# A hybrid encoder block on one core: 128-column sums and shifted work in the opening, value stores issued by ScalarE

## The chip, the core and the metric

The kernel runs on one core of a Trainium2 chip. The core has five engines that run side by side: TensorE (PE; its weight loads are listed apart as PEld), VectorE (DVE), ScalarE (ACT), GpSimd (POOL) and SyncE (SP), which only issues DMAs. Each engine works through its own queue in order and waits on semaphores for the others. The metric is the device time of one execution in microseconds; lower is better. Tiles lie in SBUF (128 partitions), TensorE writes into PSUM banks of 128 x 512 floats.

## The reference

One layer of an encoder on a sequence of 1024 positions with 1024 channels, all in float32. What bears on the change is the start of it:

```python
ada = silu(c) @ w_ada + b_ada                    # 6 x 1024 numbers from one vector c
shift1, scale1, gate1, shift2, scale2, gate2 = split(ada, 6)
h = rmsnorm(x, g_mix) * (1 + scale1) + shift1    # x: 1024 positions x 1024 channels
qa, ka, va, qb, kb, vb, ga, gb = split(h @ w_in)
oa = mixture_of_dilations(qa, ka, va)            # windows at dilations 1, 4 and 16, merged
ob = neighbourhood_attention_2d(qb, kb, vb)
x = x + gate1 * ((sigmoid(ga) * (oa @ w_branch_dil) + sigmoid(gb) * (ob @ w_branch_na)) @ w_out)
# then a second rmsnorm with shift2 and scale2, a ConvFFN, and a final rmsnorm
```

rmsnorm divides each position by the root of the mean of the squares over its 1024 channels.

## The kernel before

Activations lie transposed, channels on partitions and positions along the row, in two halves of 512 positions; a half of x is eight tiles of 128 x 512. A product in float32 precision is made of three: every operand is split into a rounded part (hi) and a rest (lo), and hi x hi, lo x hi and hi x lo are added up in PSUM. ScalarE makes hi, and GpSimd or VectorE subtracts to get lo (`split`, L57 and L61).

The part that the change touches comes first in the program, in a block with `manual_schedule`, in which the engines take their instructions in the order of the program text. Outside such blocks a planner orders them.

**The sums over channels.** A sum over the 128 partitions is a product with a column of ones. `add_sums` (L98) does this for the sums of squares, `ada_sums` (L160) for the rows of w_ada: in four products a 128 x 128 block is the stationary operand and a single column the moving one, so that one column comes out of each. In float32 every such product becomes two instructions. `warm` (L236) issues products of a 128 x 128 tile of ones with itself, whose results nobody reads; they stand between the sums.

**The opening.** c and the first half of x (8 tiles) are loaded first, then the blocks of w_ada, `wt[0]` to `wt[3]`, each of eight rows of 128 x 512, with the first weights of q, k (`qk_raw`) and v (`v_raw`) between them, and the second half of x after them, all by SP in this order. ScalarE squares the tiles of x, VectorE adds them (L452), TensorE sums over channels (`pcol`), and the reciprocal root r goes through transposes (`bcast`, L111) into a broadcast tile `pb`, which ScalarE copies to SBUF as `pbs` (L470). x is multiplied by it: tiles 0 and 1 on VectorE (L473), 2 and 3 on VectorE after the first bias (L481), 4 to 7 on GpSimd (L487).

**Rows of w_ada.** Of the eight rows of a block, some are multiplied by their number of silu(c) and added up on VectorE into one tile (`ada_rows`, L174 and L176), and that tile is summed over channels by TensorE with ones; the others go to TensorE as they are, with silu(c)'s column as the moving operand. All end in the PSUM tile `pada`.

**Four pieces.** Piece q of the loop `for q in range(4)` handles channel tiles 2q and 2q+1. `piece_bias(q)` takes the sums from `pada` (L293 adds b_ada, reading PSUM; L295 makes the scale `am1` from two SBUF operands), `scaled` makes hi and a full copy on ScalarE (L229, L230) and lo on VectorE (L231), `qk_products` (L310) adds this piece's share of q and k for the first pair of heads (12 instructions of 512 columns), and `v_parts` (L320) its share of v (24 of 256 columns). In between, VectorE works on the rows of the next block of w_ada, so that its sum is there for the next piece.

**The value stage.** After the pieces come the rest of v's first half, the second half of x (`modulate`), and the loop over `v_steps`, in which `v_wide` (L279 to L281) makes the values of 128 positions in 24 products of 512 columns into one of three PSUM banks `pv`. `v_out` copies a result to one of two SBUF tiles `vs` (ScalarE, L286) and stores it to DRAM by SP (L287). In the same loop VectorE works through the remaining blocks of w_ada in pairs of rows (`row_pairs`, L551 and L553, reloaded by L135 on SP), `row_ends` says how far by each step, and `due` when a block's sum goes to TensorE and its bias to VectorE (L167): two steps later. The fourth step splits the weights of the second branch's values, makes q and k of the second half, and copies the stored values into chunks (`va_chunks`, L408 and L410). After the loop come the sums that are left; then the buffers are freed and the attention's tables and values are loaded into them (first use of a table: L755 on GpSimd, L658 on VectorE).

The rest (attention with gates and projections beside it, branch and output projections, a ConvFFN with a seven-product scheme, the last norm) is not edited.

## Time and profile before

| what | value |
|---|---|
| plain runs, median of 3 | 1506.31 us (1505.19, 1506.31, 1511.78) |
| profiled execution, its own time | 1512.37 us |
| its span, first to last instruction | 1510.6 us |
| TensorE busy, share of the span | 1483.4 us, 98% |
| VectorE, ScalarE, GpSimd busy | 62%, 51%, 50% |
| mean granted TensorE clock | 0.992 |

Busy shares are of the whole span. For one stage one reads the timeline (start and duration of instructions, in brackets the idle time before one and what ended it), the chain of waits (the work that ended last, followed back from the end), and the stretches (busy time of an engine and the granted clock, PEclk, between two times; 1.00 is full speed). Where several instructions of a kind follow each other, a row has their count (x8), and its duration is that of all of them together. A line number can be that of a helper, so the tile's name goes with it.

### The profile page before, as it was taken

What the parts mean: (1) busy time and instruction counts of PE and PEld (TensorE: products, weight loads), DVE (VectorE), ACT (ScalarE), POOL (GpSimd) and SP (SyncE); (2) the same over time, 40 slices, a digit from 0 to 9 for tenths busy, and PEclk for the clock granted to TensorE, in tenths of its full rate; (3) what the DMA queues carried; (4) which work ended last, traced back from release to release, by engine and by line L of the source; (5) the groups of instructions that cost most, each with busy time, mean ns of one, the idle gap of its engine ahead of it and who ended that gap; (6) DMA issues with size and microseconds to landing.
All of it is one profiled execution on the core that took longest, in us unless ns stands there. A gap on an engine that the chain in (4) does not pass through costs nothing.

```text
span 1510.6 us, 21652 instructions
## 1 busy us (share of the span) xinstructions
PE 1483.4 (98%) x7664; PEld 1259.5 (83%) x7664; DVE 936.3 (62%) x1763; ACT 772.9 (51%) x1442; POOL 757.1 (50%) x633
## 2 busy tenths in 40 slices
PE   9999999999999999999999999999999999999997
PEld 8887888889798998888888778888888888777887
DVE  6684446464545665566515897666666668786765
ACT  4531666666655566653345464444444448465442
POOL 2221333433234454512268678766666676777621
PEclk8999999999999999999999999999999999999999
DMA  9477333434745555577644213222222232631323
GB/s 371 178 258 255 90 108 77 146 92 133 181 131 152 142 164 165 172 246 252 198 157 142 93 46 137 84 84 84 84 84 84 85 133 91 210 130 49 114 57 112
DMA packets 117300, 210.28 MB, mean 139 GB/s; under 512 B 42788, under 2 KB 55716, under 8 KB 117156
## 3 DMA queue, kind: packets, MB, share of 16 engines
q1 hardware_dynamic: 116632, 208.57, 43.2%
q8 instruction: 60, 0.98, 0.3%
q14 instruction: 48, 0.39, 0.1%
q10 hardware_dynamic: 560, 0.33, 0.1%
HBM read 163.58 MB, written 42.66 MB: 137 GB/s over the span
## 4 chain that ended last, share of the span: by engine, by line
PE 77%; DMA 7%; DVE 6%; POOL 4%; ACT 2%; issue 2%; SPq 0%; DVEq 0%; POOLq 0%; ACTq 0%
PE pj L1307 10%; PE pj L1306 10%; PE pj L1305 10%; PE pj L84 10%; PE pj L86 10%; PE pj L85 10%; PE pj L402 3%; PE O L1013 2%; POOL wsl L61 1%; DMA wraw<-w_down 1%; PE T L1000 1%; DMA fb<-fcs 1%; PE S L978 1%; PE O L844 1%; DMA big<-as 1%
## 5 line engine op out<-in xcount | busy, mean ns | idle before, releaser
L61 POOL TENSOR_TENSOR wlo<-wraw,whi 128x512 fp32r<-128x512 f32 (+1 forms) x96 | 118.0, 1251 | 167.6 <-ACT whi L57 152.7
L84 PE MATMUL pj<-h,whi 128*128 128x512 f32 x432 | 178.2, 413 | 0.4 <-DVE kl L374 0.4
L86 PE MATMUL pj<-h,wlo 128*128 128x512 f32 x432 | 169.8, 393 | 0.0
L85 PE MATMUL pj<-h,whi 128*128 128x512 f32 x432 | 169.4, 392 | 0.0
L1305 PE MATMUL pj<-op,wsh 128*128 128x512 f32 x408 | 159.3, 390 | 1.1 <-ACT op L1236 0.6
L1306 PE MATMUL pj<-op,wsh 128*128 128x512 f32 x408 | 158.8, 390 | 0.9 <-DVE op L1237 0.6
L1307 PE MATMUL pj<-op,wsl 128*128 128x512 f32 x408 | 158.1, 390 | 0.7 <-POOL wsl L61 0.7
L667 DVE TENSOR_TENSOR tl<-T,th 128x512 fp32r<-128x512 f32 (+3 forms) x120 | 77.1, 654 | 102.0 <-ACT th L666 100.9
L717 POOL TENSOR_TENSOR wlo<-wraw,whi 128x512 fp32r<-128x512 f32 x58 | 74.2, 1290 | 126.2 <-ACT whi L716 126.1
L61 POOL TENSOR_TENSOR wsl<-big,wsh 128x512 fp32r<-128x512 f32 (+1 forms) x86 | 113.3, 1339 | 45.2 <-ACT wsh L57 39.7
L659 ACT ACTIVATE P<-P,st 128x256 f32<-128x256 f32 x128 | 64.2, 502 | 94.2 <-DVE st L658 94.2
L1538 DVE SCALAR_TENSOR_TENSOR big<-pj,sm,big 128x512 f32<-128x512 f32 (+2 forms) x183 | 94.9, 563 | 16.5 <-ACT big L1532 15.5
L86 PEld LDWEIGHTS pj<-h,wlo 128*128 128x128 f32 x432 | 81.1, 188 | 18.1
L1305 PE MATMUL pj<-op,whi 128*128 128x512 f32 x232 | 91.3, 393 | 3.1 <-ACT whi L57 3.1
L57 ACT ACTIVATE whi<-wraw 128x1024 fp32r<-128x1024 f32 (+2 forms) x51 | 49.5, 972 | 84.2 <-DMA wraw<-w_down 32.2
L1307 PE MATMUL pj<-op,wlo 128*128 128x512 f32 x232 | 91.2, 393 | 1.3 <-POOL wlo L61 1.3
L1305 PEld LDWEIGHTS pj<-op,wsh 128*128 128x128 f32 x408 | 76.6, 188 | 18.7 <-ACT wsh L57 1.5
L1307 PEld LDWEIGHTS pj<-op,wsl 128*128 128x128 f32 x408 | 76.6, 188 | 17.9 <-POOL wsl L61 2.2
L1306 PEld LDWEIGHTS pj<-op,wsh 128*128 128x128 f32 x408 | 76.6, 188 | 17.7 <-DVE op L1237 1.3
L84 PEld LDWEIGHTS pj<-h,whi 128*128 128x128 f32 x432 | 81.5, 189 | 11.5 <-issue 0.8
L1306 PE MATMUL pj<-op,whi 128*128 128x512 f32 x232 | 90.6, 391 | 0.0
L85 PEld LDWEIGHTS pj<-h,whi 128*128 128x128 f32 x432 | 81.7, 189 | 10.1
(392 smaller groups left out, 4176.2 us busy)
## 6 DMA issues: line engine op xcount, KB each, us to landing
wraw<-w_in SPq DMA_DIRECT2D x32, 512.0 KB
wada<-w_ada SPq DMA_DIRECT2D x31, 512.0 KB
big<-w_up SPq DMA_DIRECT2D x22, 512.0 KB
wraw<-w_up SPq DMA_DIRECT2D x22, 512.0 KB
big<-as SPq DMA_DIRECT2D x22, 512.0 KB
as<-big SPq DMA_DIRECT2D x21, 512.0 KB
wraw<-w_down SPq DMA_DIRECT2D x24, 384.0 KB
gs<-gs SPq DMA_DIRECT2D x32, 256.0 KB
```

The source lines that it names most:

```text
L57: act.activation(hi, raw, AF.Copy)
L61: lo_eng.tensor_tensor(lo[:, i:i + step], raw[:, i:i + step], f(hi)[:, i:i + step], OP.subtract)
L84: pe.matmul(psum, whi[:, k0 + k], mhi, start=k == 0, stop=False)
L85: pe.matmul(psum, whi[:, k0 + k], mlo, start=False, stop=False)
L86: pe.matmul(psum, wlo[:, k0 + k], mhi, start=False, stop=k == n - 1)
L659: act.activation(pp, pp, AF.Exp, bias=mi, scale=-1.0, accum_out=li)
L667: dve.tensor_tensor(tl[:m, :n], pt[:m, :n], f(th)[:m, :n], OP.subtract)
L717: pool.tensor_tensor(lo[:, i:i + n], raw[:, i:i + n], f(hi)[:, i:i + n], OP.subtract)
L1305: pe.matmul(psum, whi[:, k], bhi, start=j < 4 and k == 0, stop=False, skip_group_check=True)
L1306: pe.matmul(psum, whi[:, k], blo, start=False, stop=False, skip_group_check=True)
L1307: pe.matmul(psum, wlo[:, k], bhi, start=False, stop=k == n - 1, skip_group_check=True)
L1538: dve.scalar_tensor_tensor(y[:, dst], src, wt, y[:, dst], OP.mult, OP.add)
```

## The change

- **Sums as 128 equal columns.** `wide_sums` does what `add_sums` and `ada_sums` do with the column broadcast to 128, so that each of the four products gives 128 equal columns; `every` reads one of each. Used for the sums of squares, for the first block of w_ada, and for the second. `pada` and `pcol` are whole banks there.
- **Order and fillers.** Rows 0 and 1 of the first block are summed right behind the squares, row 2 after the transposes. The fillers go from 35, 3, 3, 4, 2 and 5 to 38, 2 and 3.
- **One more row on TensorE.** Of the second block VectorE takes rows 0 to 4 instead of 0 to 5; row 5 goes to TensorE, between parts of the first piece's products (`qk_products` gets `parts`).
- **Inputs on GpSimd.** Tiles 2 and 3 of x are scaled by GpSimd from `pbs`, ahead of its other work in piece 0.
- **A row later.** One row of the fourth block moves from piece 1 to the start of piece 2 on VectorE.
- **Value stores.** In the loop over `v_steps` the stores are issued by ScalarE's queue (`queue=act`) instead of SP's.
- **Last sums.** The loop takes one value step more (ten instead of nine, with no rows in it), so that the sum due at step 9 stands behind that step, and the last one behind the loop.

```diff
--- before.py
+++ after.py
@@ -92,6 +92,16 @@
     ps_g = tc.alloc_tile_pool(name="psg", bufs=2, space=PSUM)
     qkpool = tc.alloc_tile_pool(name="qk", bufs=4)
 
+    def wide_sums(dst, blocks, col, first=False):
+
+        for m in range(4):
+            cc = slice(m * 128, m * 128 + 128)
+            pe.matmul(dst[:, cc], blocks[:, cc], col.to_broadcast([128, 128]), start=first and m == 0, stop=False,
+                      skip_group_check=True)
+
+    def every(p):
+        return p.rearrange("p (t c) -> p t c", c=128)[:, :, 0]
+
     def add_sums(pcol, sq, first, last, n=4):
 
         for t in range(n):
@@ -281,10 +291,10 @@
                 pe.matmul(p, hlo, whi, start=False, stop=k == KT - 1)
         return ps
 
-    def v_out(br, st, p, c0=0):
+    def v_out(br, st, p, c0=0, queue=sp):
         vs = work.tile([128, 512], FT, name="vs", bufs=2)[:, :p.shape[-1]]
         act.activation(vs, p, AF.Copy)
-        sp.dma_start((va_s, vb_c)[br][st * 128:st * 128 + 128, c0:c0 + p.shape[-1]], vs)
+        queue.dma_start((va_s, vb_c)[br][st * 128:st * 128 + 128, c0:c0 + p.shape[-1]], vs)
 
     sig = wpool.tile([128, KT], FT, name="rs", bufs=2)
     def piece_bias(q, pa):
@@ -302,10 +312,11 @@
         for raw, (hi, lo), e in zip(qk_raw, qk_w, lo_eng):
             split(raw[:, 4 * i:4 * i + 4], hi[:, 4 * i:4 * i + 4], lo[:, 4 * i:4 * i + 4], e)
 
-    def qk_products(ks):
+    def qk_products(ks, parts=range(3)):
         for k in ks:
             mhi, mlo = h[0, k]
-            for x_, (part, m) in enumerate(((0, mhi), (1, mhi), (0, mlo))):
+            for x_ in parts:
+                part, m = ((0, mhi), (1, mhi), (0, mlo))[x_]
                 for p, w in zip(qk_psum, qk_w):
                     pe.matmul(p, w[part][:, k], m, start=k + x_ == 0, stop=k == KT - 1 and x_ == 2)
 
@@ -443,42 +454,40 @@
 
         act.activation(sig, cs, AF.Sigmoid)
         dve.tensor_tensor(cs, cs, sig, OP.mult)
-        warm(35, idle, True)
+        warm(38, idle, True)
         total = early.tile([128, 512], FT, name="sq", bufs=2)
         for k in range(KT):
             sq = early.tile([128, 512], FT, name="mt", bufs=3) if k else total
             act.activation(sq, x[0][k], AF.Square)
             if k:
                 dve.tensor_tensor(total, total, sq, OP.add)
-        pcol = ps_n.tile([128, KT], FT, name="pcol")
-        add_sums(pcol, total, True, True)
-        warm(3, idle, True)
-        pa = ada_sums([(wt[0][0], cs[:, 0:1])], stop=False)
+        pcol = ps_n.tile([128, 512], FT, name="pcol")
+        wide_sums(pcol, total, ones, True)
+        pa = ps_s.tile([128, 512], FT, name="pada", bufs=1)
+        for t in range(2):
+            wide_sums(pa, wt[0][t], cs[:, t:t + 1], t == 0)
         r = wpool.tile([128, KT], FT, name="rs", bufs=2)[:, :4]
-        dve.tensor_scalar(r, pcol[:, :4], 1.0 / D, EPS, OP.mult, OP.add)
+        dve.tensor_scalar(r, every(pcol), 1.0 / D, EPS, OP.mult, OP.add)
         act.activation(r, r, AF.Sqrt)
         ada_rows(wt[0], acc, range(3, 4), 3, 7)
         dve.reciprocal(r, r)
         qk_split(0, (pool, pool))
         pb = bcast(r, ps_n, "pbc")
-        warm(3, idle, True)
-        ada_sums([(wt[0][1], cs[:, 1:2])], pa, stop=False)
-        warm(4, idle, True)
-        ada_sums([(wt[0][2], cs[:, 2:3])], pa, stop=False)
-        warm(2, idle, True)
+        wide_sums(pa, wt[0][2], cs[:, 2:3])
         pbs = early.tile([128, 512], FT, name="mt", bufs=3)
         act.activation(pbs, pb, AF.Copy)
         ada_rows(wt[0], acc, range(4, 8), 3, 7)
         for k in range(2):
             dve.tensor_tensor(x[0][k], x[0][k], pb, OP.mult)
-        ada_sums([(wt[0][7], ones)], pa)
-        warm(5, idle, True)
+        warm(2, idle, True)
+        wide_sums(pa, wt[0][7], ones)
+        warm(3, idle, True)
         for q in range(4):
             ks = range(2 * q, 2 * q + 2)
-            piece_bias(q, pa)
+            piece_bias(q, pa if q > 1 else every(pa))
             if q == 0:
                 for k in range(2, 4):
-                    dve.tensor_tensor(x[0][k], x[0][k], pb, OP.mult)
+                    pool.tensor_tensor(x[0][k], x[0][k], pbs, OP.mult)
                 stage = [ps_n.tile([128, 512], FT, name=n) for n in ("pcol", "pbc")]
             low = [scaled(x[0][k], k) for k in ks]
             if q == 0:
@@ -488,28 +497,34 @@
             if q == 1:
                 qk_split(1, (pool, pool))
                 v_split(v_raw, (pool, pool), slice(4, 8), v_w[0])
-            last = 6 if q else 5
-            steps = (range(q + 1, 4), range(4, 5), range(5, 7)) if q else (range(0), range(2), range(2, 6))
+            last = 6 if q else 4
+            steps = (range(2, 4), range(4, 5), range(5, 7)) if q else (range(0), range(1), range(1, 5))
             for some, then in zip(steps, low + [None]):
                 if q < 3:
                     ada_rows(wt[q + 1], acc, some, 0, last)
                 if then:
                     then()
             if q < 2:
-                ada_rows(wt[q + 2], acc, range(q + 2), 0, 6)
+                ada_rows(wt[q + 2], acc, range(2), 0, 6)
             if q == 2:
                 accs = sq_accs()
                 square(x[1], accs, range(4), dve)
             if q == 3:
                 v_split(v_raw1, (dve, pool), slice(0, KT), v_w[1])
                 square(x[1], accs, range(4, 8), dve)
-            qk_products(ks)
             if q == 0:
-                pa = ada_sums([(wt[1][t], cs[:, t:t + 1]) for t in (6, 7)], stop=False)
+                qk_products((0,), range(2))
+                pa = ps_s.tile([128, 512], FT, name="pada", bufs=1)
+                wide_sums(pa, wt[1][5], cs[:, 5:6], True)
+                qk_products((0,), range(2, 3))
+                qk_products((1,))
+                for t in (6, 7):
+                    wide_sums(pa, wt[1][t], cs[:, t:t + 1])
                 v_parts(0, range(4), ks, (0,))
-                ada_sums([(wt[1][5], ones)], pa)
+                wide_sums(pa, wt[1][4], ones)
                 v_parts(0, range(4), ks, (1, 2))
                 continue
+            qk_products(ks)
             v_parts(0, (0,), ks, range(3))
             if q < 3:
                 pa = ada_sums([(wt[q + 1][7], cs[:, 7:8])], stop=False)
@@ -537,7 +552,7 @@
         for t, raw in enumerate(v_raws[1]):
             sp.dma_start(raw, w_in[22 + t])
         v_steps = [(0, 4, 5), (0, 6), (0, 7), None] + [(1, st) for st in range(8)]
-        row_ends = (4, 7, 10, 12, 14, 17, 19, 22, 24)
+        row_ends = (4, 7, 10, 12, 14, 17, 19, 22, 24, 24)
         sums = {}
 
         def row_pairs(n0, n1):
@@ -575,7 +590,7 @@
 
         done_rows = 0
         due = {}
-        for n, step in enumerate(v_steps[:9]):
+        for n, step in enumerate(v_steps[:10]):
             if step is None:
                 for ks in (slice(0, 4), slice(4, 8)):
                     for hv in range(2):
@@ -595,7 +610,7 @@
             row_pairs(done_rows, row_ends[n])
             if step is not None:
                 for st, pp in zip(step[1:], p):
-                    v_out(step[0], st, pp)
+                    v_out(step[0], st, pp, queue=act)
             for j in due.pop(n, ()):
                 ada_bias(4 * j, ada_sums([(sums.pop(j), ones)]))
             due[n + 2] = [j for j in range(4, 10) if done_rows < 4 * j - 12 <= row_ends[n]]
@@ -626,7 +641,7 @@
         return vv
 
     first_w = w_split(ahead.pop(1), pool)
-    for br, st in v_steps[9:]:
+    for br, st in v_steps[10:]:
         v_out(br, st, *v_wide(st))
     work.release()
     ps_s.release()
```

## The prediction

> **What bounds the kernel now.** I read the page first, then the chain of waits over the first 300 us, then the granted clock by stretches, then the order of instructions where the change lies.
>
> ```profile
> span 1510.6 us, 21652 instructions
> PEclk8999999999999999999999999999999999999999
> ```
>
> The span is 1510.6 us; the profiled execution took 1512.37 us (1.8 us lie around the span), and the median of the three plain runs is 1506.31 us (one of them took 1511.78). I make the sum against the profiled execution and carry the difference, in us, over to the median. The clock row says where to look: TensorE has its full clock in every slice but the first. The chain of waits there (start, us, what):
>
> ```profile
> 11.30 1.05 PE pcol L98 x8
> 12.35 0.78 PE pv L236 x6
> 13.13 0.79 PE pada L160 x8
> 13.92 0.49 PE pbc L111 x4
> 14.41 1.21 PE pv L236 x6
> 15.62 1.50 PE pada L160 x8
> 17.12 1.92 PE pv L236 x8
> 19.03 1.50 PE pada L160 x8
> 20.53 1.06 PE pv L236 x4
> 21.59 1.50 PE pada L160 x8
> 23.09 2.34 PE pv L236 x10
> 25.43 4.02 PE pj L310 x12
> ...
> 52.30 2.93 PE pj L310 x12
> 55.23 2.87 PE pv L320 x24
> ```
>
> From 11.30 to 25.43 the chain is TensorE alone: one-column sums (L98, L160) with filling products (L236) between them. The same eight instructions of L160 cost 0.79 us at 13.13 and 1.50 at 15.62, and twelve products of L310 cost 4.02 at first and 2.93 later. The granted clock tells why (stretch, PE busy and count, PEclk, DMA):
>
> ```profile
> 10.95:14.36 3.41, 3.06 (x28) 1.00 1.03 401
> 14.36:17.77 3.41, 3.41 (x19) 0.50 1.00 339
> 17.77:21.19 3.42, 3.42 (x18) 0.50 1.02 417
> ...
> 38.26:41.67 3.41, 3.41 (x29) 1.00 1.04 397
> ```
>
> The clock is halved from 14.36 on, and its steps come in stretches of 3.41 us. In the stretch before the fall, instructions of 128 columns or more fill 0.78 us (L236) to 1.27 us (with the transposes of L111), 23 to 37%; the rest is one-column work and 0.35 us of idleness. At 38.26 the clock holds although one-column sums take some 1.75 us (next fence, 39.56 and 40.37): 49% is left. So the clock falls at 23 to 37% of columned work in such a stretch and holds at 49%.
>
> The Trainium skill ("TensorE: Matmul & The Clock Gate", the section on the HAM clock gate) has windows of 3413 ns, and its table of advice asks for no idle gap over some 3 us. The window agrees with the 3.41 us steps; the gap does not: the trace idles 0.35 us in that window and the clock falls all the same.
>
> **The opening, step by step.** Rows of the timeline (start, us, engine, line, tiles, count, idle time before):
>
> ```profile
> 1.07 9.52 PE L236 MATMUL pv<-om 128*128 128x128 f32 x70 [1.07 <-DVE om L119]
> 15.25 2.50 POOL L61 TENSOR_TENSOR wlo<-wraw,whi 128x512 fp32r<-128x512 f32 x2 [14.82 <-DMA wraw<-w_in]
> 16.37 1.28 DVE L473 TENSOR_TENSOR ks<-ks,pbc 128x512 f32<-128x512 f32 x2
> 23.13 0.17 DVE L293 TENSOR_TENSOR ada<-pada,sm 128x4 f32<-128x4 f32 x1 [5.47 <-PE pada L160]
> 23.33 0.16 DVE L295 SCALAR_TENSOR_TENSOR am<-ada,sm 128x2 f32<-128x2 f32 x1
> 27.69 2.33 DVE L176 SCALAR_TENSOR_TENSOR pv<-wada,cs,pv 128x512 f32<-128x512 f32 x3
> 32.02 2.53 POOL L487 TENSOR_TENSOR qb<-qb,mt 128x512 f32<-128x512 f32 x2
> 33.21 1.35 DVE L295 SCALAR_TENSOR_TENSOR am<-ada,sm 128x2 f32<-128x2 f32 x1
> 34.60 0.81 ACT L229 ACTIVATE h<-ks,ada,am 128x512 fp32r<-128x512 f32 x1 [7.11 <-DVE am L295]
> 35.47 0.74 PE L310 MATMUL pj<-h,whi 128*128 128x512 f32 x2 [0.47 <-ACT h L229]
> 39.56 0.95 PE L160 MATMUL pada<-cs,wada 128*128 128x1 f32 x8
> 40.37 1.03 PE L160 MATMUL pada<-ones,wada 128*128 128x1 f32 x8
> 44.13 0.74 PE L310 MATMUL pj<-h,whi 128*128 128x512 f32 x2 [0.47 <-ACT h L229]
> ```
>
> *A wide sum.* No row shows a sum with a 128-column broadcast operand. Nearest: a filler at 128 columns, 0.78 us for six, 0.13 each at most (0.11 where they run dense), and a one-column sum, 1.05 for eight, 0.13. I take 0.11, the rate of the same form, so 0.89 us for the eight instructions of one row block; at 0.13 it is 1.05. So at full clock a wide sum is no dearer than a narrow one, and it counts as columned work. The opening's fillers go from 35+3+3+4+2+5 to 38+2+3 products, two instructions each; the last of the first batch now ends about 11.1 and fills the idleness before 11.30.
>
> *TensorE, at full clock.* Sums of squares from 11.30, 0.89: 12.2. Two rows of w_ada, 1.78: 14.0 (the r chain of DVE and ACT hides beside them, as it does beside L236 and L160 now). Transposes 0.49: 14.5. Third row 0.89: 15.4. Two fillers 0.45: 15.8. Then TensorE waits for DVE's last row of the first block, which ends at 16.37 (there L473 starts), and sums it from 16.5 to 17.4. Three fillers: 18.05.
>
> *piece_bias(0).* DVE is free at 17.65 (16.37 plus 1.28), the sum is there at 17.6: L293 at 17.7, L295 ready at 17.9. Here the change meets itself. L295 takes 0.16 us with GpSimd idle, but 1.35 at 33.21, and ends exactly where GpSimd's pair from 32.02 ends (34.55). L293, which reads PSUM, keeps its 0.17 beside a busy GpSimd. The change puts two more products (x[0][2], x[0][3], 1.27 us each by L487) on GpSimd right behind wlo, so from 17.75 to 20.3; I let L295 wait for the first of them: it ends 19.05 (bounds: 18.05 with no wait, 20.3 behind both). ScalarE follows at 19.1 and the first product 0.87 us later (34.60 to 35.47): 20.0, against 25.1 now.
>
> The Trainium skill ("SBUF — State Buffer", the section on the two separate sides) names an exclusive lock between GpSimd and a VectorE operation with two SBUF inputs, held for the whole instruction. The 1.35 us agree; by it the wait is certain, as I assume. It speaks against this edit.
>
> *What leaves DVE.* Two products of L481, of the kind of L473 (0.64 each), and one row of w_ada (0.78 by L176) in piece 0. DVE is waiting for TensorE at 23.13 (5.47 us idle), so the first hide wholly; the row takes 0.78 from the path to the second bias and costs TensorE 0.89. In the later pieces one row moves from behind piece 1's rows to before piece 2's, where DVE waits for ScalarE: nothing, at worst 0.78.
>
> *Piece 0 on TensorE.* 2.93 (pj) + 2.87 (pv) + four wide blocks at 0.89 = 9.4 us: 20.0 to 29.4. The second L295 waits the same way behind x[0][4] to [7] on GpSimd (by then 25.3 to 30.4), and should end near 29.1; the first product of piece 1 starts near 30.0, against 35.47. That is **5.5 us**. Piece 1's rows need no later weights, since the loads keep their order and times. In front of piece 2 TensorE idles 0.47 us for L229 (44.13); with DVE 0.78 earlier relative to it, this goes: **6.0 us** in all. Pieces 2 and 3 then run on TensorE as now.
>
> **The value stage.** Rows around it (engine, line, idle time before and what ended it):
>
> ```profile
> 116.98 7.89 SPq L135 DMA_DIRECT2D wada<-w_ada  x4
> ...
> 131.11 0.33 SPq L287 DMA_DIRECT2D vbc<-vs  x1
> 136.13 0.60 ACT L286 ACTIVATE vs<-pv 128x512 f32<-128x512 f32 x1 [6.82 <-DMA vbc<-vs]
> 136.78 0.50 PE L279 MATMUL pv<-vwh,h 128*128 128x512 f32 x1 [0.50 <-ACT vs L286]
> 140.05 1.02 PE L160 MATMUL pada<-ones,sq 128*128 128x1 f32 x8 [0.92 <-DVE ada L167]
> 151.39 1.01 POOL L755 TENSOR_TENSOR bias<-bias,lnm 128x384 f32<-128x384 f32 x1 [19.48 <-DMA vv<-v]
> 158.41 0.42 DVE L658 CUSTOM_DVE_ANT_0 P<-S,bias 128x256 f32<-128x256 f32 x1 [11.50 <-PE S L770]
> ```
>
> Value stores stand on SP behind loads of w_ada; a store lands late, ScalarE waits for its buffer (136.13), and TensorE for the bank (136.78): 0.50 us. Issued by ScalarE itself, a store goes out right after the eviction. It then stands in ScalarE's order: queued behind it are the next eviction and the splits. Its price is 0.33 us by the store at 131.11, up to 1.97 where SP's issues are held (7.89 for four); with 0.60 for the eviction that is under 2.6 us in a step of 24 products, 5 us on TensorE, so it hides; if the cover went, ten times 0.33 is 3.3. SP loses ten issues, so the loads of w_ada move up a little. The last-but-one sum comes one value step later, which covers the 0.92 us at 140.05; the last sum then meets DVE's last row early, and I give 0.1 back. So 0.50 + 0.92 - 0.1 = **1.3 us** (0 to 1.4). Nothing past that is touched, and the stage runs on TensorE in between, so the 6.0 us carry.
>
> **Sum.** 6.0 + 1.3 = 7.3 us: 1506.3 - 7.3 = **1499.0 us** (1505.1 for the profiled execution). 0.5% is 7.5 us, about what a measurement of this kernel can tell from no change; the forecast lies at this edge. The forecast's own range, from the L295 bounds (+1 to -2.5), the wide sum's price (up to -1) and the second stage (0 to 1.4), is 1497.5 to 1503.
>
> **Rivals.** *The clock falls later.* The change leaves two holes, 15.8 to 16.5 and 18.05 to 20.0. A stretch of 3.41 us laid over both has 1.45 to 1.56 us of columned work, 43 to 46%, between the 37% that fell and the 49% that held, and nearer to the latter. If it falls, near 20, it comes back after one or two stretches, since piece 0 is dense (at 25.09 in the present kernel dense products raised it in one): 3.4 to 6.8 us at half rate cost 1.7 to 3.4 us, of which 0.6 hides behind L295. With 2.3 lost: 1501.3. Chance 0.24.
>
> *The clock falls and stays (slower).* The low stretches at 14.36 and 17.77 show that fillers mixed with one-column sums keep it down. Should piece 0, with its waits, stay below what raises it, its 9.4 us take 18.8, piece 1 starts at 38.8 + 0.6 = 39.4, 3.9 later than now, and piece 1 (8.66 us from 35.47 to 44.13), if it runs low for two thirds, loses another 5.8: 9.7 - 1.3 = 8.4 slower, 1514.7. It decides from where the clock isn't back by some 31 us. For it: one-column sums remain in piece 1. Against it: dense products raised it before. Chance 0.07.
>
> *The last sum holds up the attention.* Its tables load only when the last sum has freed the buffers; the table is ready at 152.4 (151.39 + 1.01) and first used at 158.41, 6.0 us of slack. One value step (5 us) fits; if the sum is laid behind two (10 us), TensorE waits 4: 1503.0. The stores or stalls of the value stage not moving at all gives 1500.3. Chance of these 0.14.
>
> The Trainium skill's advice on gaps (same section as above) would let no hole of 1.9 us lower the clock, on the forecast's side; the fall at 14.36 came with less idleness than that, so I give it no weight.
>
> **How the numbers follow.** Forecast 0.55. Faster by over 0.5%: half of 0.55 less a little, and a sliver of the second case, 0.30. Slower by over 0.5%: the third case, with noise, 0.07. The rest 0.63. The range takes the forecast's bounds, widened by 2.5 us below for a stage that gains more than its rows show, and above to the second and fourth cases and nearly to no gain: 1495 to 1506. As the time I give the forecast's, 1499.0.
>
> **What would show it.** Right: PEclk 1.00 from 4 us on, first L310 near 20 and the one of piece 1 near 30; L295 twice above 1 us, ending with a GpSimd product; no TensorE wait for vs near 130 or for ada near 134. Wrong: PEclk 0.50 anywhere between 14 and 40 (rivals), L295 short, a first softmax that waits for the table, or more than 1 us of TensorE idleness for vs or for a store held on ScalarE.

## The result, and the profile after

| | before | after |
|---|---|---|
| median of 7 runs | 1506.85 us (1505.19 to 1511.78) | 1500.62 us (1499.54 to 1503.41) |
| ratio of the two | | 0.9959, 95% interval 0.9946 to 0.9972 |
| profiled execution, and its span | 1512.37 us, 1510.6 us | 1499.64 us, 1497.8 us |

The forecast was 1499.0 us, and it is 1.6 us off. Its reasons held far less well than its number, as a second profile of each kernel shows. First the profile after, from its page:

```profile
span 1497.8 us, 21627 instructions
PEclk9999999999999999999999999999999999999999
```

The first slice of the clock row is 9 now and was 8. The opening in the timeline (start, us, engine, line, tiles, count, idle time before and what ended it); L303, L305, L239 and L321 of the changed kernel are L293, L295, L229 and L310 of the kernel before, and L99 is the wide sum:

```profile
17.74 2.50 POOL L490 TENSOR_TENSOR ks<-ks,mt 128x512 f32<-128x512 f32 x2
18.15 0.87 DVE L305 SCALAR_TENSOR_TENSOR am<-ada,sm 128x2 f32<-128x2 f32 x1
19.93 0.73 PE L321 MATMUL pj<-h,whi 128*128 128x512 f32 x2 [1.34 <-ACT h L239]
21.78 1.57 PE L99 MATMUL pada<-cs,wada 128*128 128x128 f32 x8 [0.66 <-DMA wada<-w_ada]
23.00 2.05 PE L321 MATMUL pj<-h,whi 128*128 128x512 f32 x4
27.24 0.75 DVE L184 TENSOR_SCALAR pv<-wada,cs 128x512 f32<-128x512 f32 x1 [1.53 <-DMA wada<-w_ada]
30.21 0.16 DVE L305 SCALAR_TENSOR_TENSOR am<-ada,sm 128x2 f32<-128x2 f32 x1
31.72 0.63 PE L321 MATMUL pj<-h,whi 128*128 128x512 f32 x2
```

Piece 0 starts at 19.93 (20.0 was forecast), piece 1 at 31.72 (30.0). In between TensorE waits 0.66 us for a row of the second block of w_ada that is still under way, and four products at 23.00 take 2.05 us, at half clock. VectorE's wait of 1.53 us is for the third block, which piece 1 does not need; it hides, since VectorE's bias of piece 1 (L303, at 30.01) then waits 1.23 us more for TensorE's sum.

In a second profile of the changed kernel (the run after_again) the clock is full here, and what holds piece 1 back is VectorE's L305, which waits for GpSimd a second time:

```profile
28.85 2.52 POOL L496 TENSOR_TENSOR qb<-qb,mt 128x512 f32<-128x512 f32 x2
29.06 1.10 DVE L305 SCALAR_TENSOR_TENSOR am<-ada,sm 128x2 f32<-128x2 f32 x1
31.12 0.73 PE L321 MATMUL pj<-h,whi 128*128 128x512 f32 x2 [0.38 <-ACT h L239]
```

L305 ends at 30.16, where the first product of GpSimd's pair ends, and the first product of TensorE follows 0.96 us later.

Now the same start of the pieces in the kernel *before*, profiled a second time (the run before_again):

```profile
20.27 0.74 PE L310 MATMUL pj<-h,whi 128*128 128x512 f32 x2
...
30.08 0.73 PE L310 MATMUL pj<-h,whi 128*128 128x512 f32 x2
```

These are the marks forecast for the changed kernel, without the change: 20.27 and 30.08, against 25.09 and 35.47 in the first profile. In this execution the clock is full from 4.95 us to 1380.5. The halved clock of the first profile, on which the 6.0 us of the opening rest, did not come in this one. Of the five profiles below with the old opening, two have 13.65 us at half clock from 14.3 (before, act_queue_only), two have 6.83 us from 26.16 and 27.45 (last_sums_only, value_only), and one has none. Of the eight with the new opening and its wide sums, only the first profile of the changed kernel has any in its opening, 3.41 us.

All profiles at three marks (us; "pieces" is the start of the last value product of the pieces, "S" the first product of the attention). The last two columns are late, in the stage that multiplies by w_down: the time between ScalarE's tenth-last and last split of a weight's high half (whi, L57), and TensorE's waits from 1290 to 1445 us by the waits view.

| run | pieces | S | S minus pieces | late stretch | late waits |
|---|---|---|---|---|---|
| before | 57.8 | 157.6 | 99.8 | 140.3 | 7.1 |
| before_again | 52.4 | 152.4 | 100.0 | 139.8 | 7.2 |
| act_queue_only | 56.9 | 157.8 | 100.8 | 139.4 | 6.8 |
| last_sums_only | 53.8 | 152.6 | 98.8 | 138.0 | 7.0 |
| value_only | 53.7 | 151.6 | 97.9 | 138.2 | 6.6 |
| no_pool_fill | 51.8 | 149.7 | 97.9 | 138.0 | 7.5 |
| no_pool_fill_again | 51.3 | 149.2 | 97.9 | 139.7 | 7.6 |
| after | 52.5 | 150.4 | 97.9 | 134.7 | 4.6 |
| after_again | 52.2 | 150.2 | 98.0 | 134.1 | 4.3 |
| open_only | 52.2 | 152.0 | 99.9 | 134.7 | 4.5 |
| no_pool | 52.2 | 150.1 | 97.9 | 134.7 | 4.6 |
| narrow | 52.4 | 150.3 | 97.9 | 135.2 | 4.3 |
| row_back | 52.2 | 150.1 | 97.9 | 133.5 | 4.0 |
| row_no_pool | 51.7 | 149.7 | 97.9 | 135.6 | 5.1 |

The two second profiles differ by 7.9 us of span (1504.7 and 1496.8): 0.2 by the end of the pieces, 2.0 in the value stage, and 5.7 in the late stretch, which the change does not touch in the code. The 0.2 holds for this pair alone: over all profiles the pieces end at 52.4 to 57.8 with the old opening (mean 54.9) and at 51.3 to 52.5 with the new one and wide sums (mean 52.0).

### The profile page after: what moved, and what is told of

It is laid out like the page before. It is cut to its first block, busy times and chain, and to the rows that moved or that the text cites. A ratio compares the mean times of both kernels' runs of the same rounds, so it can differ in the third digit from the quotient of the medians.

```text
span 1497.8 us, 21627 instructions
## 1 busy us (share of the span) xinstructions
PE 1475.4 (99%) x7654; PEld 1253.4 (84%) x7654; DVE 934.0 (62%) x1760; ACT 774.0 (52%) x1442; POOL 761.1 (51%) x635
## 4 chain that ended last, share of the span: by engine, by line
PE 82%; DMA 7%; POOL 5%; DVE 4%; issue 1%; ACT 1%; SPq 1%; DVEq 0%; POOLq 0%; ACTq 0%
PE pj L1322 10%; PE pj L1321 10%; PE pj L1320 10%; PE pj L84 10%; PE pj L86 10%; PE pj L85 10%; PE pj L413 2%; PE O L1028 2%; DMA fb<-fcs 2%; PE T L1015 1%; POOL wsl L61 1%; PE S L993 1%; PE pv L289 1%; PE pv L291 1%; PE pv L290 1%
## 5 line engine op out<-in xcount | busy, mean ns | idle before, releaser
L1320 PE MATMUL pj<-op,wsh 128*128 128x512 f32 x408 | 159.4, 391 | 1.2 <-ACT op L1251 0.6
L1322 PE MATMUL pj<-op,wsl 128*128 128x512 f32 x408 | 157.8, 390 | 0.0
L682 DVE TENSOR_TENSOR tl<-T,th 128x512 fp32r<-128x512 f32 (+3 forms) x120 | 77.2, 654 | 101.1 <-ACT th L681 99.9
L57 ACT ACTIVATE whi<-wraw 128x1024 fp32r<-128x1024 f32 (+2 forms) x51 | 49.5, 973 | 83.8 <-DMA wraw<-w_down 30.9
L1320 PEld LDWEIGHTS pj<-op,wsh 128*128 128x128 f32 x408 | 76.6, 188 | 19.1 <-ACT wsh L57 2.0
L1322 PE MATMUL pj<-op,wlo 128*128 128x512 f32 x232 | 90.4, 390 | 2.0 <-POOL wlo L61 2.0
L1320 PE MATMUL pj<-op,whi 128*128 128x512 f32 x232 | 90.8, 391 | 1.1 <-ACT whi L57 1.1
L1321 PEld LDWEIGHTS pj<-op,wsh 128*128 128x128 f32 x408 | 76.6, 188 | 17.6 <-DVE op L1252 1.3
L1322 PEld LDWEIGHTS pj<-op,wsl 128*128 128x128 f32 x408 | 76.6, 188 | 16.3 <-POOL wsl L61 0.5
```

The lines of the kernel that those rows point to most:

```text
L57: act.activation(hi, raw, AF.Copy)
L682: dve.tensor_tensor(tl[:m, :n], pt[:m, :n], f(th)[:m, :n], OP.subtract)
L1320: pe.matmul(psum, whi[:, k], bhi, start=j < 4 and k == 0, stop=False, skip_group_check=True)
L1321: pe.matmul(psum, whi[:, k], blo, start=False, stop=False, skip_group_check=True)
L1322: pe.matmul(psum, wlo[:, k], bhi, start=False, stop=k == n - 1, skip_group_check=True)
```

## The experiments

Theory A is that of the prediction: columned sums and filled holes keep the clock up in the opening. Theory B: parts of the opening are hidden, and the time comes from elsewhere. The kernel before ran beside each group, with a median of 1507.38 us beside the first four experiments, 1507.06 beside the next four and 1508.47 beside the last four.

**narrow**

```diff
-            pe.matmul(dst[:, cc], blocks[:, cc], col.to_broadcast([128, 128]), start=first and m == 0, stop=False,
+            pe.matmul(dst[:, m * 128:m * 128 + 1], blocks[:, cc], col, start=first and m == 0, stop=False,
```

> The changed kernel with its sums taken back to one column each: same order, same fillers, same rows on TensorE, same work on GpSimd, same value stage; only the moving operand of wide_sums is 1 column instead of 128. Theory (the gain of the opening is the clock, held up by columned sums): PEclk falls to 0.50 between 14 and 18 us as in the kernel before and stays there until dense products of piece 0 raise it; first product of piece 0 near 20.5 to 21.5 (19.9 with wide sums, since VectorE's row and the wait for GpSimd hide part), piece 1 at 34 to 36 (31.7), so 2.5 to 4 us of the 6.2 are lost: ratio near 0.998. Rival (the gain is the shorter order with nine fillers fewer, and the clock matters little): piece 1 within 0.5 us of 31.7, ratio 0.996 as with wide sums.

Measured: 1505.06 us, ratio 0.9983 (0.9972 to 0.9995), mean clock 0.991 over 12 runs against 0.996 of the changed kernel. By the medians the columns are worth 4.4 us, by the two ratios to the kernel before 3.6. The time is the one that the theory of the clock expected; the marks of the profile are those of the rival, with the first two pieces starting at 20.23 and 31.48. The clock is halved from 15.12 to 21.94 and again from 28.77 to 32.18. For the second fall, the timeline and the stretches (PE busy and count, PEld, DVE, ACT, POOL, then PEclk, DMA share, GB/s):

```profile
24.74 1.84 PE L99 MATMUL pada<-cs,wada 128*128 128x1 f32 x16
26.44 1.21 PE L331 MATMUL pv<-vwh,h 128*128 128x256 f32 x8
27.49 0.95 PE L99 MATMUL pada<-ones,wada 128*128 128x1 f32 x8
28.30 1.67 PE L331 MATMUL pv<-vwh,h 128*128 128x256 f32 x8
```

```profile
25.36:28.77 3.41, 3.41 (x31) 3.41 (x32) 2.28 (x5) 0.00 (x0) 3.41 (x4) 1.00 1.02 407
28.77:32.18 3.41, 3.41 (x17) 3.31 (x16) 3.17 (x6) 2.95 (x5) 1.59 (x2) 0.50 1.03 386
```

The clock falls at 28.77 behind a stretch without any idleness: of the 3.41 us from 25.36, L331 has 1.05 (26.44 to 27.49) and 0.47 (from 28.30), 45%, and one-column sums the rest. In the one profile the two low stretches hide behind waits (pieces 52.4), so the 4.4 us are the median's, not this execution's, and no profile shows where they go.

In the changed kernel the stretch ahead of the fall at 22.31, and in its second profile one that held:

```profile
18.90:22.31 3.41, 1.73 (x9) 1.24 (x10) 1.80 (x4) 3.25 (x5) 1.34 (x2) 1.00 1.03 410
22.31:25.72 3.41, 3.41 (x13) 2.83 (x12) 3.29 (x5) 0.73 (x2) 3.13 (x3) 0.50 1.05 392
```

```profile
17.46:20.87 3.41, 1.83 (x14) 1.64 (x14) 2.79 (x5) 0.49 (x1) 2.87 (x3) 1.00 1.02 414
```

Columned work (here all of PE's busy time) of 1.73 us (51%) let it fall, 1.83 us (54%) kept it. But the share alone does not decide. In before_again a stretch without idleness held the clock as well:

```profile
15.71 1.14 PE L236 MATMUL pv<-om 128*128 128x128 f32 x8
17.49 0.69 PE L236 MATMUL pv<-om 128*128 128x128 f32 x4
```

```profile
15.19:18.60 3.41, 3.41 (x32) 3.41 (x33) 2.41 (x4) 1.12 (x2) 2.51 (x2) 1.00 0.99 353
```

Its fillers have 0.97 us (15.71 to 16.68) and 0.53 (17.49 to 18.02), 44%, and one-column sums the rest. So 44, 49 (the stretch from 38.26 in the prediction) and 54% held, 45 and 51% fell. What differs from run to run is where the stretches' borders lie. The same opening has them at 10.95 and 14.36 in before, with 23 to 37% of columned work between them, and at 11.78 and 15.19 in before_again, with 55% (1.88 us): the clock fell in the first and held in the second.

**value_only** (the kernel before, with both edits of the value stage)

```diff
-                    v_out(step[0], st, pp)
+                    v_out(step[0], st, pp, queue=act)
...
-        row_ends = (4, 7, 10, 12, 14, 17, 19, 22, 24)
+        row_ends = (4, 7, 10, 12, 14, 17, 19, 22, 24, 24)
...
```

> The kernel before with the value stage's edits alone (stores issued by ScalarE, last sums one step later), the opening as before. Theory (two separate gains that add): the opening's marks as before (first product 25, piece 1 at 35.5, pieces end at 57.8), TensorE's waits of 0.66 and 1.08 us near 137 and 140 gone, first S product at 155.7 to 156.1 instead of 157.6; 1505.0 to 1505.4, ratio 0.9988. Rival (the value stage gains only because the earlier opening puts its loads at other times): the waits stay or move, S within 0.5 us of 157.6, ratio 1.000.

Measured: 1505.78 us, ratio 0.9993 (0.9977 to 1.0008). S minus pieces fell from 99.8 to 97.9, both waits are gone, so the stage is worth 1.9 us by its marks; the medians cannot tell that from no change. The old opening here took 53.7 us, at full clock until 27.45: the first sign that the half clock from 14.36 does not always come.

**open_only** (the changed kernel, with the value stage as before)

```diff
-                    v_out(step[0], st, pp, queue=act)
+                    v_out(step[0], st, pp)
...
-        row_ends = (4, 7, 10, 12, 14, 17, 19, 22, 24, 24)
+        row_ends = (4, 7, 10, 12, 14, 17, 19, 22, 24)
...
```

> The changed kernel with the value stage's edits undone (stores by SP, nine steps in the loop). Theory: pieces as in the changed kernel (end at 52.4), TensorE's two waits come back (0.66 and 1.08, near 131 and 135), S at 152 to 152.3; 1502.0, ratio 0.9968. Rival: with the opening earlier the waits vanish by themselves, S at 150.4, ratio 0.996.

Measured: 1501.4 us, ratio 0.9964 (0.9951 to 0.9977). The value stage takes 99.9 us again. Against value_only the start of the attention is later (152.0 and 151.6), yet the kernel is 4.4 us faster: something behind the attention distinguishes the two.

**no_pool**

```diff
                 for k in range(2, 4):
-                    pool.tensor_tensor(x[0][k], x[0][k], pbs, OP.mult)
+                    dve.tensor_tensor(x[0][k], x[0][k], pb, OP.mult)
```

> The changed kernel with tiles 2 and 3 of x scaled by VectorE again, behind the first bias. Theory A (the wait of L305 behind GpSimd lies on the path): L305 short (0.16 instead of 0.87), first product of piece 0 near 19.2 instead of 19.9, and pieces 1 to 3 0.7 us earlier (31.0, 38.7, 46.1). Theory B (it is hidden, since TensorE then waits 0.66 us at 21.8 for row 5 of the second block to be loaded): first product 19.2, but piece 1 at 31.5 to 31.9 and the rest as before. The times differ by less than the runs can tell; the marks decide.

Measured: 1498.17 us, ratio 0.9948 (0.9933 to 0.9963). L305 takes 0.16 us instead of 0.87, and the first product starts at 20.03 instead of 19.93. The two do not compare directly: VectorE's bias (L303) came at 18.77 here and at 17.96 there. In after_again it came at 18.90, L305 took 1.25 us, and the first product started at 21.25. So the wait costs about 1.2 us at the first product, and nothing at piece 1 (31.09, against 31.12 in after_again), where L305 waits for GpSimd's other tiles in both: 1.23 us from 28.96 here.

**row_back** (row 5 of the second block on VectorE, as before)

```diff
-            last = 6 if q else 4
-            steps = (range(2, 4), range(4, 5), range(5, 7)) if q else (range(0), range(1), range(1, 5))
+            last = 6 if q else 5
+            steps = (range(2, 4), range(4, 5), range(5, 7)) if q else (range(0), range(2), range(2, 6))
...
-                wide_sums(pa, wt[1][5], cs[:, 5:6], True)
...
-                wide_sums(pa, wt[1][4], ones)
+                wide_sums(pa, wt[1][5], ones)
```

> The changed kernel with row 5 of the second weight block back on VectorE (four steps of the chain instead of three, and no eight products for it on TensorE); all else as in the changed kernel. The row matters (theory A): VectorE's chain for the second block is what piece 1 waits for, so the first product of piece 1 comes one step of 0.75 us later than in the changed kernel, near 32.4 (31.8 in a run without a halved clock), and the time is some 0.7 us up. The row is hidden (theory B): TensorE reached the row at 21.78 only when its load had landed, and VectorE's last step of that block ends at 25.7, while the closing sum of the block begins at 28.9 behind products of piece 0; so 0.76 us more on VectorE end before it, TensorE loses its wait of 0.66 and 1.1 to 1.6 us of products, and the first product of piece 1 comes at the same time or up to 1.5 us earlier, 30.2 to 31.7; time within 1.0 us of the changed kernel's.

Measured: 1498.25 us, ratio 0.9938 (0.9921 to 0.9955). Piece 1 starts at 31.10, not near 32: the row on TensorE buys nothing. L305 again waits for GpSimd, from 29.21 to 30.14, and TensorE is idle for 1.40 us ahead of piece 1, so what it saves cannot show.

**no_pool_fill** (no_pool, and six fillers more)

```diff
-        warm(3, idle, True)
+        warm(9, idle, True)
```

> The changed kernel with two edits: tiles 2 and 3 of the input are scaled on VectorE behind the first bias (as in the run before), and the filler behind the closing sum of the first block is nine products instead of three, 1.7 us instead of 0.8, so that TensorE has no hole before the first product of piece 0. Theory that the holes let the clock fall: the opening is at full clock in every execution, the mean clock of the runs is 0.997 or more, the time spreads by less than 3 us and its median is some 1 us under that of the changed kernel, 1497 to 1499. Theory that the columns alone hold the clock, and the hole does nothing: times and clocks as in the run without GpSimd's tiles, 1498.2 with a spread to 1502.8 from stretches late in the kernel. Should the fillers themselves stand in the way of the first product, it comes later than 20.03.

Measured: 1503.31 us, ratio 0.9972 (0.9960 to 0.9984). Both theories fell. The opening is the earliest so far (S at 149.7), and by the medians the kernel is 5.1 us slower than no_pool, from which it differs by six fillers in a time when TensorE waits; by the ratios it is 3.6 us, and their intervals just overlap. The two profiles differ in the late stretch, 138.0 us against 134.7. (Their spans are only 0.7 us apart, since the profiled execution of no_pool, 1502.63 us, ran at half clock for 6.83 us from 1464.43.)

**act_queue_only** and **last_sums_only** (the first and the second edit of value_only, each alone)

> The kernel before with one edit: the value stores are issued by ScalarE; sums and opening as before. From the end of the pieces to the first product of the attention the kernel before took 99.8 us, the kernel with both edits of the value stage 97.9. If it is the stores in SyncE's queue that hold up the later weights and so cost the 1.9 us, this kernel takes 97.9 and loses both waits of TensorE (0.66 at 136.8 and 1.08 at 140.1). If it is the place of the last sums, it takes 99.8 and keeps both. If each edit takes one of the waits, 98.7 to 99.2. In time, 0 to 2 us under the kernel before.

> The kernel before with the other edit alone: the last row sums of the value stage one step later; stores and opening as before. If the stores in SyncE's queue cost the 1.9 us, the stretch from the end of the pieces to the first product of the attention stays at 99.8 us, or the wait comes back somewhat later, behind the same load; if it is the place of the sums, it takes 97.9. If each edit takes one of the two waits, 98.7 to 99.2. In time, 0 to 2 us under the kernel before.

Measured: 1506.86 us, ratio 0.9999 (0.9984 to 1.0014), and 1505.13 us, ratio 0.9987 (0.9973 to 1.0002). TensorE's waits from 60 to 152 us, of before_again, act_queue_only and last_sums_only (in value_only and after_again the view is empty):

```profile
PE pada L160 <- DVE ada L167: 1.0, 1, 1.0
PE pv L279 <- ACT vs L286: 0.6, 1, 0.6
```

```profile
PE pada L160 <- DVE ada L167: 1.1, 1, 1.1
```

```profile
PE pv L279 <- ACT vs L286: 0.5, 1, 0.5
```

Each edit takes one wait, as the prediction had it, though neither median can be told from the kernel before. That act_queue_only needs 100.8 us for the stage all the same goes with a clock that falls at 140.64, behind the wait that it keeps.

**row_no_pool** (both edits of row_back and no_pool)

> Both edits that were faster than the changed kernel by their medians: row 5 of the second block back on VectorE, and tiles 2 and 3 scaled on VectorE. If each took something of its own from the opening (theory A), the first product of piece 1 comes before the 31.1 of either and the median goes below 1498, to 1497. If both hide behind the load of the second block and the medians differ by the clock's low stretches and the late waits alone (theory B), the pieces start at 20.0 and 31.1, the first product of the attention at 150.1, and the time is between 1497.5 and 1500.5.

Measured: 1500.5 us, ratio 0.9945 (0.9923 to 0.9967). Pieces at 19.58 and 30.63, 0.4 earlier than in either, S at 149.7, and no faster than either (1498.2). The mark is that of theory A and the time that of theory B: 0.4 us in the opening are lost again behind it, in a profile with 5.1 us of late waits and low stretches at 393, 1376 and 1465 us.

**before_again** and **after_again** (both kernels unchanged)

> The kernel before, unchanged, profiled a second time. Theory that the halved clock in its opening depends on a phase that changes from run to run: the low stretch lies at another place or is shorter than the 13.65 us from 14.36, and the start of the attention comes between 153.5 (an opening as in the run of the old opening with the new value stage, 20.7 and 53.7, and 99.8 for the value stage) and 157.6. Theory that the old opening halves the clock always there, and the value edits kept it up: again 13.65 us from 14.4 and the attention at 157.6.

> The changed kernel, unchanged, profiled a second time. Theory of the phase: the low stretch of 3.41 us at 22.31 moves or is missing, and then piece 1 starts near 31.1 instead of 31.72; the attention starts within 0.4 us of 150.3 all the same. Theory that something in the new opening makes it fall there: again 3.41 us near 22.3 and piece 1 at 31.7.

Measured: 1506.44 and 1498.56 us, one execution each. Once risen (at 4.95 and 7.22 us), the clock has no low stretch in either opening. S came at 152.4, even earlier than expected of the kernel before, and at 150.2.

**no_pool_fill_again**

> The run with nine fillers and no tiles on GpSimd in the opening, profiled a second time. In the first profile its opening was the earliest of all (attention at 149.71) and its end one of the latest of the new openings (span 1501.5), from 3.08 us of waiting for a split weight near 1379.6 and a low stretch at 1467.1. Theory that the late waits and stretches come and go from run to run: attention again at 149.7, another sum of waits between 1300 and 1400, a low stretch elsewhere or none, and a span that differs by over 1 us. Theory that an earlier arrival makes the late loads collide: the same wait of about 3 us near 1379, and a span within 1 us of 1501.5.

Measured: 1505.09 us, one execution. Span 1503.3, 1.8 more than at first, but again 7.6 us of late waits (7.5 at first): they came in both executions, while the low stretches of the clock differ (one at 1467, and here three, from 393.73, 1380.18 and 1468.92).

## Where the late microseconds go

TensorE's waits from 1281 to 1421 us, in before_again, after_again and no_pool_fill_again (L1320 and L1322 are L1305 and L1307 of the kernel before):

```profile
PE pj L1305 <- ACT whi L57: 4.4, 4, 1.6
PE pj L1307 <- POOL wlo L61: 1.3, 1, 1.3
PE pj L1307 <- POOL wsl L61: 1.1, 2, 0.7
PE pj L1305 <- ACT wsh L57: 0.4, 1, 0.4
```

```profile
PE pj L1320 <- ACT whi L57: 1.9, 3, 0.8
PE pj L1322 <- POOL wlo L61: 1.5, 1, 1.5
PE pj L1320 <- ACT wsh L57: 0.7, 2, 0.4
PE pj L1322 <- POOL wsl L61: 0.2, 1, 0.2
```

```profile
PE pj L1320 <- ACT whi L57: 4.8, 4, 1.6
PE pj L1322 <- POOL wlo L61: 1.3, 1, 1.3
PE pj L1322 <- POOL wsl L61: 0.8, 1, 0.8
```

The difference between these is the waits for whi, and whi waits for a load. Timelines of the three, in the same order:

```profile
1373.31 1.51 SPq L1419 DMA_DIRECT2D wraw<-w_down  x2
1378.78 0.84 ACT L57 ACTIVATE whi<-wraw 128x768 fp32r<-128x768 f32 x1 [3.66 <-DMA wraw<-w_down]
1379.68 0.50 PE L1305 MATMUL pj<-op,whi 128*128 128x512 f32 x1 [1.60 <-ACT whi L57]
```

```profile
1370.10 1.52 SPq L1434 DMA_DIRECT2D wraw<-w_down  x2
1373.66 0.85 ACT L57 ACTIVATE whi<-wraw 128x768 fp32r<-128x768 f32 x1 [1.74 <-DMA wraw<-w_down]
```

```profile
1371.33 1.52 SPq L1434 DMA_DIRECT2D wraw<-w_down  x2
1376.85 0.84 ACT L57 ACTIVATE whi<-wraw 128x768 fp32r<-128x768 f32 x1 [3.69 <-DMA wraw<-w_down]
1377.75 0.50 PE L1320 MATMUL pj<-op,whi 128*128 128x512 f32 x1 [1.63 <-ACT whi L57]
```

No slower engine is in this, only a load that lands later. Two loads of 384 KB are issued 0.98 us apart, and the split waits for the first: 5.5 us from its issue to the split in the first and the third, 3.6 in the changed kernel. What the transfer of the two met is told by the DMA view, in 40 slices of 0.125 us; first before_again from 1374 to 1379, then after_again from 1371 to 1376:

```profile
GB/s 0 0 0 0 0 111 123 135 160 86 147 197 270 369 381 344 307 295 307 307 332 463 332 320 332 344 270 123 62 74 61 0 12 12 12 12 25 25 25 25
...
q1 hardware_dynamic: 541, 0.78, 50.8%
q8 instruction: 1, 0.02, 1.2%
```

```profile
GB/s 0 0 0 86 147 209 147 111 197 147 283 344 393 381 369 320 320 344 356 381 393 406 381 295 209 74 0 0 0 0 0 0 0 0 0 0 0 0 0 0
```

An instruction fetch (q8, one packet of 16 KB, 0.98 us from 1376.7) falls into the loads. Behind it the rate falls to 12 to 25 GB/s for over a microsecond: the last small packets pass one after another, each 0.07 us, where the loads of the other kernel are through at 1374.3. The trace tells the landing of each load in 16 parts. In before_again 15 parts of the first load have landed at 1377.01 and the last at 1378.76; in after_again all 16 have landed at 1373.64, 3.5 us after the issue. It looks as if the fetch held up the one part that shared its way; which way that was no view shows. In no_pool_fill_again the fetch starts at 1374.8, 3.5 us behind the first issue. Some 90 us earlier the same fetch series meets a reload: GpSimd's first product on it (wc from big) waits 2.32 us for the load in before_again, 0.34 in after_again and 1.57 in no_pool_fill_again.

The late load is only half of it. Behind the wait the clock falls in before_again, which it does not in after_again:

```profile
1380.52:1383.93 3.41, 2.17 (x5) 1.79 (x6) 3.08 (x5) 3.41 (x8) 3.41 (x5) 0.50 0.00 0
1383.93:1387.35 3.42, 3.42 (x9) 2.64 (x9) 1.69 (x3) 3.25 (x6) 2.86 (x4) 0.50 0.00 0
```

Product for product, TensorE in before_again is 2.0 us behind after_again at 1292.6, 5.0 us at 1379.7, where the wait ends, and 7.4 us at 1387.0: 3.0 us are lost by waits and 2.4 at half clock. The clock falls at this place in six of the upper seven profiles of the table, for 3.41 or 6.83 us, and in three of the lower seven, for 3.41.

Over all 14 profiles the two groups do not overlap. In the upper seven of the table a fetch starts 3.1 to 3.6 us behind the first issue of the pair of loads near 1374, and the second of the two lands 5.05 to 5.52 us after its issue; in the lower seven it lands after 3.58 to 4.34. The first load lands late in three of the upper seven (5.45 to 5.55 us); in the other four TensorE waits at the next step, 2.9 us for wlo, which GpSimd makes behind its first work on the second. In the upper seven another fetch starts 2.3 to 4.6 us behind the tenth-last split of whi; in the lower seven none falls into the pair of loads, and the other comes 6.0 to 7.3 us behind the split. The step from the tenth-last to the ninth-last split takes 18.6 to 19.7 us in the upper seven, 17.6 to 18.0 in the lower.

What puts the fetches there is the number of TensorE instructions ahead. The program has 7484 products in the kernel before and 7485 in no_pool_fill, but 7479 in the changed kernel and no_pool, and 7475 in row_back. The q8 fetches follow that count: 60 of them to 15328 products and weight loads in before_again, some 255 to each, and 27 to 34 us apart in this stage. The fetch that falls into the loads comes with 1235 to 1239 of these instructions left to the end in the upper seven; the one of that place in the lower seven, behind the loads, with 1209 to 1217. Five f32 products are twenty instructions, since each runs as two weight loads and two products (35 of them in the program are x70 in the trace); at the 0.11 us of an instruction in the dense stage I estimate that as 2.2 us of a fetch's place. The Trainium skill ("Runtime: NRT & Kernel Launch", Terms) says that each engine's instruction memory is refilled in blocks of 16 KiB; the trace agrees for q8 (60 packets of together 0.98 MB), while the other instruction queue, q14, has 48 packets of together 0.39 MB, some 8 KB each.

How much is shown: that six fillers in a wait cost 5.1 us by the medians, and that time is lost where loads land later with a fetch in their transfer and in the half clock that follows, is measured. That the wait brings the half clock about is likely from their order, and not shown. That the fetch alone does it, without the fillers, was not tried: taking five fillers from the kernel before should give it the late stretch of the changed one, and no run here has that.

## Why the prediction was right, and where not

- **The first product at 20.0 (measured 19.93; 21.25 in the second profile).** Right for the changed kernel, wrong as a gain. The failed step is "against 25.1 now": the profiled execution took 6.06 us more than the median shown beside it, and I carried its difference over to that median in us. With the clock full, the old opening gives 20.27 and ends its pieces at 52.4, 0.2 us behind the new one. What the new opening does is to hold the clock more often: one of eight profiles with it has half clock there, against four of five with the old one, and over these its pieces end 2.9 us earlier on average, not 6.0. The mean clock of the whole kernel agrees, with 0.996 over 7 runs against 0.994 over 29 of the kernel before.
- **L295 waits for GpSimd.** Right for the first, within its bounds: 0.87 us, ending at 19.02 where a product of the pair at 17.74 ends, and in the second profile 1.25 us, ending at 20.35 behind both products. The edit costs about 1.2 us at the first product there, and nothing at piece 1 (no_pool). The second L305 waited in one profile (1.10 at 29.06) and not in the other (0.16, where the half clock had brought it late).
- **Piece 1 at 30.0, and the row worth 0.78.** Measured 31.72 and 31.12. In the first profile the failed step is that piece 1's rows "need no later weights": TensorE waited 0.66 us for one, and half clock took the rest. In the second it is the end of the second L305, put near 29.1: it ended at 30.16, one of GpSimd's products later, and piece 1 hangs on it. It ends so at 30.14 to 30.19 in row_back and no_pool too, which start the piece at 31.10 and 31.09, so the row is worth nothing.
- **The rival of a clock that falls later** (near 20, back after one or two stretches) came true in the first profile, for one stretch from 22.31, and not in the second. The two differ by 0.6 us at piece 1 and 0.2 at the end of the pieces, less than the 2.3 given. The rule behind it, that the clock falls at 23 to 37% of columned work and holds at 49%, did not stand: 51% and 45% fell, and 44% held. The Trainium skill's limit on gaps ("TensorE: Matmul & The Clock Gate", the section on the HAM clock gate) does not fit this trace: the longest gap ahead of that fall is 1.34 us.
- **The value stage, 1.3 us (0 to 1.4).** The mechanism was right, edit by edit; the size is 1.9 to 2.0. The two waits alone are 1.6 in before_again, against the 0.50 and 0.92 that I added; some 0.4 us stays open.
- **A store on ScalarE costs 0.33 to 1.97 us and hides.** It hides, and each issue takes the 0.33 us of the lower bound. But a store need not go out right after its eviction, as the prediction had it: in the changed kernel the store behind the eviction at 112.74 went out at 121.72, 8.4 us after that eviction ended (what held it no run shows):

```profile
112.74 0.60 ACT L296 ACTIVATE vs<-pv 128x512 f32<-128x512 f32 x1 [5.79 <-PE pv L291]
121.72 0.33 ACTq L297 DMA_DIRECT2D vbc<-vs  x1
```

- **"Nothing past that is touched", and so "the 6.0 us carry".** This failed, and made up for the first point; that the two errors cancel to 1.6 us is luck. What carries between two undisturbed openings is 0.2 + 2.0 us, and 5.7 us come 1.1 ms later, some 3 us of them as waits for loads, behind fetches that the smaller number of TensorE instructions has shifted, and 2.4 as half clock. How the 6.2 us between the medians divide among the opening's clock, the value stage and the late stretch, no run shows.

Faster than the changed kernel by their medians are row_back (1498.25) and no_pool (1498.17), but their ratios' intervals overlap that of the changed kernel.

## What to carry to other kernels

Look at two profiles before calling a low clock a property of the code: compare the profiled time with the median first, and where it is far off, price the step by the undisturbed rate. A gain that is predicted early is only confirmed by marks all along the kernel; here, with both openings at full clock, the marks after the edited stages showed 2.2 us, and the other 5.7 came from elsewhere. When a few instructions more or fewer in a waiting engine move the end by microseconds, look at where the instruction fetches fall among the loads that bound a later stage.

## What the runs showed of the hardware

- With an instruction fetch of 16 KB in the midst of two loads of 384 KB, the second of them landed 5.05 to 5.52 us after its issue, without it 3.58 to 4.34. Six fillers, placed where TensorE waited, moved the fetch there, and cost 5.1 us by the medians some 1.3 ms later.
- The clock fell behind a 3.41-us stretch with 45% columned work and no idleness, and behind one with 51% and the rest idle; it held at 44% without idleness, at 49% and at 54%. The stretches' borders differ from run to run, and with them whether one opening runs at half clock for 13.65 us or not at all.
- The 0.16-us VectorE operation that makes the scale (L295, L305 after the change) took up to 1.35 us where it came in the midst of a GpSimd product, and ended with one.
- A store issued by ScalarE stayed 8.4 us in its queue, and TensorE had no wait from 60 to 152 us in that profile.
